# A two-layer hybrid decoder trunk on one core: banks for the latent values, side work in six pieces, and half of layer 2's value weights prepared at the end of layer 1

## The chip, the core and the metric

The kernel runs on one core of a Trainium2 chip. A core has a matrix engine (TensorE, PE), a vector engine (VectorE, DVE), a scalar engine (ScalarE, ACT) and a general engine (GpSimd, POOL); SyncE (SP) issues the DMA transfers here. TensorE writes its results to eight accumulation banks (PSUM), and a bank can take the next result only when the engines that read the last one are done. Each engine works through its own instructions in a fixed order. The metric is the time of one execution on the device, in microseconds (us); less is better.

## What is computed

A sequence of 1024 tokens with 16 learned meta tokens ahead of it (1040 columns in the kernel) goes through two layers. Each layer normalises its input, projects it, runs three kinds of attention beside each other, gates and merges them, and adds an output projection:

```python
def hybrid_layer(x, pos, norm_g, w_in, b_f, g_cq, g_ckv, w_uq, w_ukv, sinks, w_branch, w_out):
    h = rmsnorm(x, norm_g)
    proj = h @ w_in
    (a_q, a_k, a_v, a_f, a_z, b_cq, b_ckv, b_kr, b_z,
     c_q, c_k, c_v, c_z, gates) = jnp.split(proj, np.cumsum(SPLIT_SIZES)[:-1], axis=-1)
    log_f = jax.nn.log_sigmoid((a_f + b_f).astype(jnp.float32))
    log_cum = jnp.cumsum(log_f, axis=1)                    # the forget gate
    y_a = causal_block_attention(a_q, a_k, a_v, FOX_DH ** -0.5, log_cum)
    cq = rmsnorm(b_cq, g_cq)                               # the latent norms
    ckv = rmsnorm(b_ckv, g_ckv)
    qB = (cq @ w_uq)
    kvB = (ckv @ w_ukv)                                    # latent keys and values
    k_rope = rope(b_kr, pos)                               # the shared rotary key
    y_b = causal_block_attention(q_b, k_b, v_b, (MLA_NOPE + MLA_ROPE) ** -0.5)
    y_c = sliding_window_sink_attention(rope(c_q), rope(c_k), c_v, sinks)
    ...
    return x + merged @ w_out
```

The model is 1024 wide; the latent key and value part has 256 channels, the latent query part 384.

## The kernel before

All matrices are 32-bit floats. For TensorE each is split into a rounded high part and the remainder, and each product is three matmuls: high by high, high by low, low by high (`mm3`, L175 to L177; for values L453 to L455). A split of a weight is `split` (L157 and L158): a cast on ScalarE (`wh`, `wvh`) and a subtraction (`wl`, `wvl`) on GpSimd; for activations the subtraction is VectorE's. `weights` loads 1024 columns into a buffer `wr` and splits them; there are two buffers `wr` for all weights, `value_weights` (the weights of the value projections, of 320, 360 and 256 columns for each of the input's 128-row parts, in pieces of up to 1024 columns) uses the same two.

The eight banks are four tags of two: ps_s, ps_pj, ps_t and ps_o. `dense()` gives the next bank out of a rotation, `banks[0]`, which is MOST (ps_s and ps_pj) or ALL (all four). A norm takes its sum of squares and its reciprocal root on ps_t (`rstd`, L189 to L204) and its products on ps_o (`normed`, L212), whatever the rotation is.

A layer goes through these stages:

- **Values.** `values` runs over the eight token blocks of 128 (t) and, for each, over two halves (`wv0`, 320 columns, then `wv1`, 360 columns, which also hold the shared rotary key and the forget gate); at the end over the meta tokens. ScalarE copies the first half to `vst` (L460), VectorE the second (L458), and SyncE stores them.
- **Sliding-window keys and queries, and side work.** The key projection T_CK, then four query columns in two passes (kv). Ahead of pass 0 stand `forget_gates`, ahead of pass 1 `rotary_key` (L550 to L588): small operations of VectorE, ScalarE and SyncE on 8 and 32 rows, for the forget gate's running sum (scans L582, offsets L585, additions L587) and the shared key's rotation.
- **The latent stage.** Projections to the latent channels, their two norms, then `values(vb, 1, ...)` on the normed channels, sixteen blocks of six matmuls of 256 columns, with gate projections (`some`) between; then the latent keys (`wkn`), four pairs in three chunks of 264, 264 and 512 columns. From the end of the norms on the rotation is ALL (`banks[0] = ALL`, ahead of L674).
- Attention, gates, merge. Then the **output projection**: eight columns (d) of three chunks, each followed by the addition of the residual (L1023), its squares and a store to `x_d`. The last two columns are run chunk by chunk, and after each chunk comes the norm of layer 2. Layer 2 then begins with `value_weights` of both halves and `values`.

The order in which an engine gets its instructions is not the program's. A scheduler runs through the program with its own timing and gives each engine the ready instruction that is first in the program; the result is fixed, and on the chip each engine takes it in that order.

Of the kernel before, what the change touches and what calls it, by code (L numbers as in the profile page):

```python
# [11 lines left out]
F32 = mybir.dt.float32  # L12
F32R = mybir.dt.float32r
# [5 lines left out]
P = 128  # L19
# [66 lines left out]
def tile_kernel(ctx: ExitStack, tc, a, out):  # L86
# [320 lines left out]
    def value_weights(pool, srcs, nk, raws=None):  # L407

        ws = []
        for i, src in enumerate(srcs):  # L410
            n = src.shape[1]
            ncol = n // nk
            wh = pool.tile([P, n], F32R, tag=f"wvh{i}", name="wvh")
            wl = pool.tile([P, n], F32R, tag=f"wvl{i}", name="wvl")
# [12 lines left out]
    def values(pool, which, ws, nk, rh, rl, rest=None, between=None):  # L427
# [7 lines left out]
        for t in list(range(NB)) + [-1]:  # L435
            rows = NM if t < 0 else P
            s0 = 0 if t < 0 else NM + t * P
            for half, (wh, wl, ncol) in enumerate(ws):
                o = dense()[:, :ncol]
                st = pool.tile([P, 360], F32, tag="vst", name="vst", bufs=4)  # L440
                if t < 0:
                    for k in range(nk):
                        for i, w in enumerate((wh, wl)):
                            nc.tensor.matmul(o[:48], xm[:, k], w[:, k * ncol:(k + 1) * ncol],
                                             start=(k + i == 0), stop=(k == nk - 1 and i == 1))
                    nc.scalar.copy(st[:NM, :ncol], o[32:48])
                    nc.vector.tensor_tensor(st[:NM, :ncol], o[:NM], st[:NM, :ncol], ALU.add)
                    o = st
                else:
                    for k in range(nk):  # L450
                        xh = rh[:, k, s0:s0 + P]
                        w1 = wh[:, k * ncol:(k + 1) * ncol]
                        nc.tensor.matmul(o, xh, w1, start=(k == 0), stop=False)  # L453
                        nc.tensor.matmul(o, xh, wl[:, k * ncol:(k + 1) * ncol], start=False, stop=False)
                        nc.tensor.matmul(o, rl[:, k, s0:s0 + P], w1, start=False, stop=(k == nk - 1))  # L455
                nv = ncol // DH * DH
                if t >= 0 and half:
                    nc.vector.tensor_copy(st[:, :nv], o[:, :nv])  # L458
                elif t >= 0:
                    nc.scalar.copy(st[:, :nv], o[:, :nv])  # L460
                dma(vm_d[which][:, 2 * half:2 * half + 2] if t < 0 else v_d[which][half, :, t],
                    st[:rows, :256])
                if nv > 256:
                    dma(vc_d[:rows, t + 1, half], st[:rows, 256:320])
# [688 lines left out]
```

## Time and profile before

| | |
|---|---|
| median of 3 runs | 2605.56 us (2605.33 to 2613.88) |
| profiled execution, its own time | 2608.11 us |
| its span, first to last instruction | 2606.3 us |
| TensorE busy | 2535.9 us, 97% |
| VectorE, ScalarE, GpSimd busy | 49%, 46%, 38% |
| mean granted TensorE clock | 0.990 |

The span is that of one profiled execution; 1.8 us of its time lie outside the span. A matmul's busy time is modelled, so two matmuls that follow each other closely overlap in the timeline; their distance is told by their starts. In a timeline the bracket at the end of a row says how long the engine was idle ahead of it, and what ended that.

### The profile page before, as it was taken

The numbers are of one execution on the slowest core, as the hardware profiler recorded it, in microseconds if no ns is written. First come the engines' busy times: TensorE is split into PE (matmuls) and PEld (weight loads), VectorE is DVE, ScalarE is ACT, GpSimd is POOL, SyncE is SP. The second block draws the span as 40 slices with busy tenths as digits, with TensorE's granted clock in tenths as the row PEclk, the third lists the DMA queues.
The fourth block names the chain that finished last, engine by engine and source line by source line (L and its number), as shares of the span: only waits on it lengthen the run. The fifth ranks groups of instructions, "written<-read, shape, count | busy, mean of one in ns | idle before, by whom it ended". The sixth has DMA issues, their size and how long they took to land.

```text
span 2606.3 us, 42099 instructions
## 1 busy us (share of the span) xinstructions
PE 2535.9 (97%) x15446; PEld 2263.1 (87%) x15446; DVE 1283.8 (49%) x3339; ACT 1199.7 (46%) x2684; POOL 993.8 (38%) x966
## 2 busy tenths in 40 slices
PE   8999999999999999999999989999999999999998
PEld 7888899999888999899988878888887888888797
DVE  6464355544263445657156453455334623565643
ACT  5233355545374456644232333455445633566433
POOL 2141545354332424462333325445324341352534
PEclk9999999999999999999999989999999999999999
DMA  5143512222634434364232344222216353453532
GB/s 168 54 136 137 202 46 81 76 74 80 172 103 112 128 102 126 105 223 167 87 101 79 116 156 159 70 82 70 86 69 172 106 158 86 117 148 122 178 130 73
DMA packets 137631, 303.40 MB, mean 116 GB/s; under 512 B 22560, under 2 KB 63296, under 8 KB 137424
## 3 DMA queue, kind: packets, MB, share of 16 engines
q1 hardware_dynamic: 137424, 300.71, 37.5%
q8 instruction: 122, 2.00, 0.3%
q14 instruction: 85, 0.70, 0.1%
HBM read 211.98 MB, written 88.66 MB: 115 GB/s over the span
## 4 chain that ended last, share of the span: by engine, by line
PE 85%; DMA 5%; DVE 5%; ACT 2%; issue 1%; SPq 1%; POOL 1%; POOLq 0%; ACTq 0%; DVEq 0%
PE ps_pj L175 15%; PE ps_pj L176 15%; PE ps_pj L177 15%; PE ps_t L268 5%; PE ps_s L982 3%; PE ps_o L312 3%; PE ps_s L176 3%; PE ps_s L177 3%; PE ps_s L175 2%; PE ps_o L310 2%; PE ps_o L175 2%; PE ps_t L177 2%; PE ps_t L175 2%; PE ps_t L176 2%; PE ps_o L176 2%; PE ps_o L177 2%
## 5 line engine op out<-in xcount | busy, mean ns | idle before, releaser
L158 POOL TENSOR_TENSOR wl<-wr,wh 128x1024 fp32r<-128x1024 f32 (+1 forms) x156 | 373.8, 2397 | 798.1 <-ACT wh L157 667.5
L175 PE MATMUL ps_pj<-hh,wh 128*128 128x512 f32 (+1 forms) x1912 | 672.5, 352 | 5.0 <-DVE zs L718 2.2
L176 PE MATMUL ps_pj<-hl,wh 128*128 128x512 f32 (+1 forms) x1912 | 671.1, 351 | 0.0
L177 PE MATMUL ps_pj<-hh,wl 128*128 128x512 f32 (+1 forms) x1912 | 669.6, 350 | 0.0
L175 PEld LDWEIGHTS ps_pj<-hh,wh 128*128 128x128 f32 x1912 | 362.3, 189 | 47.7 <-DVE zs L718 3.0
L177 PEld LDWEIGHTS ps_pj<-hh,wl 128*128 128x128 f32 x1912 | 362.6, 190 | 41.1 <-issue 0.2
L176 PEld LDWEIGHTS ps_pj<-hl,wh 128*128 128x128 f32 x1912 | 362.4, 190 | 39.9 <-issue 0.5
L158 DVE TENSOR_TENSOR ptl<-ps_t,pth 128x512 fp32r<-128x512 f32 (+1 forms) x386 | 244.7, 641 | 139.3 <-ACT pth L157 132.9
L157 ACT CAST pth<-ps_t 128x512 fp32r<-128x512 f32 (+1 forms) x386 | 205.9, 547 | 170.1 <-PE ps_t L268 140.9
L260 ACT ACTIVATE P<-P,mn 128x656 f32<-128x656 f32 (+8 forms) x272 | 206.9, 761 | 163.9 <-DVE mn L255 159.2
L157 ACT CAST wh<-wr 128x1024 fp32r<-128x1024 f32 (+1 forms) x156 | 162.1, 1039 | 250.4 <-PE ps_pj L176 146.2
L268 PE MATMUL ps_t<-ident,P 128*128 128x128 f32 x1152 | 188.0, 276 | 0.8 <-DVE ptl L158 0.7
L310 PE MATMUL ps_o<-pth,vp 128*128 128x256 f32 (+1 forms) x640 | 167.6, 277 | 2.6 <-DVE u L281 1.4
L312 PE MATMUL ps_o<-ptl,vp 128*128 128x256 f32 (+1 forms) x640 | 159.7, 287 | 2.1 <-DVE ptl L158 1.9
L298 POOL COPY pmeta<-P 128x16 f32<-128x16 f32 x256 | 49.7, 198 | 273.7 <-ACT P L260 270.1
L982 PE MATMUL ps_s<-kt,qt 96*128 96x328 f32 (+9 forms) x696 | 147.8, 330 | 2.9 <-DVE mn L255 2.7
L268 PEld LDWEIGHTS ps_t<-ident,P 128*128 128x128 f32 x1152 | 135.3, 141 | 9.2 <-DVE ptl L158 1.5
L792 POOL TENSOR_TENSOR cm<-ckb,tri 128x128 f32<-128x128 f32 (+1 forms) x136 | 60.5, 447 | 184.9 <-DVE mn L255 181.2
L310 PEld LDWEIGHTS ps_o<-pth,vp 128*128 128x128 f32 x640 | 120.8, 189 | 11.3 <-ACT pth L157 1.9
L312 PEld LDWEIGHTS ps_o<-ptl,vp 128*128 128x128 f32 x640 | 120.5, 188 | 8.8 <-DVE ptl L158 4.7
L281 DVE TENSOR_TENSOR u<-ps_o,hv 64x256 f32<-64x256 f32 x128 | 53.9, 421 | 136.6 <-ACT hv L280 121.5
L982 PEld LDWEIGHTS ps_s<-kt,qt 96*128 96x128 f32 (+1 forms) x696 | 109.2, 188 | 10.1 <-DVE mn L255 5.3
(391 smaller groups left out, 5667.2 us busy)
## 6 DMA issues: line engine op xcount, KB each, us to landing
wr<-in_w_dram SPq DMA_DIRECT2D x108, 512.0 KB
gate_d<-gt SPq DMA_DIRECT2D x72, 256.0 KB
gt<-gate_d SPq DMA_DIRECT2D x24, 520.0 KB
wr<-in_wbr_dram SPq DMA_DIRECT2D x24, 512.0 KB
gt<-gate_d SPq DMA_DIRECT2D x24, 512.0 KB
kn_d<-sg SPq DMA_DIRECT2D x16, 520.0 KB
ckb<-ck_d SPq DMA_DIRECT2D x16, 520.0 KB
kt<-kn_d SPq DMA_DIRECT2D x16, 520.0 KB
```

The costliest lines, as they stand in the source:

```text
L157: nc.scalar.copy(hi, src)
L158: (eng or nc.vector).tensor_tensor(lo, src, _f(hi), ALU.subtract)
L175: nc.tensor.matmul(dst, w1, rh[:, k, c0:c1], start=(k == 0), stop=False)
L176: nc.tensor.matmul(dst, w1, rl[:, k, c0:c1], start=False, stop=False)
L177: nc.tensor.matmul(dst, wl[:, k * P:k * P + m], rh[:, k, c0:c1], start=False, stop=(k == nk - 1))
L260: nc.scalar.activation(s[:rows, :n], s[:rows, :n], AF.Exp, bias=prev, scale=-1.0, accum_out=total)
L268: nc.tensor.transpose(t[:kk, c:c + rows], src, ident[:rows, :rows])
L281: nc.vector.tensor_tensor(u[mine, :n], o[mine, :n], t[mine, :n], ALU.add)
L310: nc.tensor.matmul(dst, vp[:, j + x, vs], ph[:, cols], start=(j + x == 0), stop=False)
L312: nc.tensor.matmul(dst, vp[:, j + x, vs], pl[:, cols], start=False, stop=(diag and x == 1))
L792: nc.gpsimd.tensor_tensor(cm[:rows, :rows], ckb[:rows, d:n], tri[:rows, :rows], ALU.add)
L982: nc.tensor.matmul(dst, q[:, qi, q0:q0 + rows], kt[:, ki, c0:c1], start=(x == 0), stop=(x == 2))
```

## The change

Four things are changed:

- The rotation stays at MOST while the latent values and the latent keys are computed; it becomes ALL after them.
- `forget_gates` and `rotary_key` are one generator, `side_work`, with five stops. One piece is written into the program after each query chunk, the rest after the loop.
- The weights wv0 of layer 2 are loaded and split in the program after column d = 2 of layer 1's output projection, into a pool `vw` of their own that is allocated behind hh and hl and released with layer 2's query stage. Layer 2's start then prepares wv1 alone.
- `values` has its inner part in `block(t, half)`, and with span 2 (layer 2's first values) its order is t0 first half, t1 first half, t0 second half, t1 second half, and so on. The turn of the small columns that each block leaves is taken first in, first out.

```diff
-        for t in list(range(NB)) + [-1]:
+        def block(t, half):
...
-                if half == 0 and due:
-                    due.pop()()
+            if half == 0 and due:
+                due.pop(0)()
...
+        for ts in [range(t, t + span) for t in range(0, NB, span)] + [[-1]]:
+            for half in range(len(ws)):
+                for t in ts:
+                    block(t, half)
+                    if between and half and t % 3 == 1:
+                        between()
...
-            ws = value_weights(va, [a["wv0"][l], a["wv1"][l]], KD)
+            ws = early_ws + value_weights(va, [a["wv1"][l]], KD, at=1)
...
-        values(va, 0, ws, KD, hh, hl, rest)
+        values(va, 0, ws, KD, hh, hl, rest, span=1 if first else 2)
...
-        def rotary_key():
+        def side_work():
...
             nc.scalar.activation(e, e, AF.Ln, bias=ones[:H, 0:1])
+            yield
...
+                if n_ == 4:
+                    yield
+            yield
...
             dma(ck_d, e)
+            yield
...
+            nc.vector.tensor_tensor(r2, krt[32:64], s16[32:64], ALU.mult)
+            yield
...
             for kv in range(2):
-                (rotary_key if kv else forget_gates)()
...
                         split(rows[x][0][:, c0:c1], rows[x][1][:, c0:c1], oo[x], SWA_SCALE)
+                    next(aside, None)
...
+            for _ in aside:
+                pass
         pa.release()
+        if not first:
+            vw.release()
...
-        banks[0] = ALL
 
         with tc.tile_pool(name=f"mq{l}", bufs=2, side=A, reuse_waits="tile") as pm:
             values(vb, 1, ws, 2, cvh, cvl, between=some)
...
                 some()
+            banks[0] = ALL
...
             hl = hpool.tile([P, KD, L], F32R, tag="hl", name="hl")
+            vw = tc.alloc_tile_pool(name=f"vw{l}", bufs=1, side=A, reuse_waits="tile")
...
                     column(d, w, c0, c1)
+                if first and d == 2:
+                    early_ws = value_weights(vw, [a["wv0"][l + 1]], KD)
```

Lines below the values are up to twenty further down in the changed kernel; L453 to L455 become L454 to L456, L458 becomes L459.

The first place is SyncE's queue at the end of layer 1, from the first store of the output projection on. `in_wo_dram` are output weights, `in_wv_dram` layer 2's value weights, `x_d` the stores. Before:

```order
L101 DMA x_d<-xn 128x264
L101 DMA wr<-in_wo_dram 128x1024
L101 DMA x_d<-xn 128x264
L101 DMA x_d<-xn 128x512
L101 DMA x_d<-xn 128x264
L101 DMA wr<-in_wo_dram 128x1024
L101 DMA x_d<-xn 128x264
L101 DMA x_d<-xn 128x512
L101 DMA x_d<-xn 128x264
L101 DMA wr<-in_wo_dram 128x1024
```

and now:

```order
L101 DMA x_d<-xn 128x264
L101 DMA wr<-in_wv_dram 128x960
L101 DMA x_d<-xn 128x264
L101 DMA x_d<-xn 128x512
L101 DMA x_d<-xn 128x264
L101 DMA wr<-in_wv_dram 128x960
L101 DMA x_d<-xn 128x264
L101 DMA wr<-in_wv_dram 128x640
L101 DMA x_d<-xn 128x512
L101 DMA wr<-in_wo_dram 128x1024 x2
```

The three loads of wv0 take the places of the next two wo loads and one more, and two wo loads follow right behind the third; one store of 512 columns stands between.

The second place is the start of layer 2 on TensorE; 320 columns are a first half, 360 a second. Before, the rows around the first matmul of a second half:

```order
L454 MATMUL ps_s<-wvl,hh 128x320
L455 MATMUL ps_s<-wvh,hl 128x320
L453 MATMUL ps_s<-wvh,hh 128x320
L454 MATMUL ps_s<-wvl,hh 128x320
L453 MATMUL ps_pj<-wvh,hh 128x360
L455 MATMUL ps_s<-wvh,hl 128x320
L453 MATMUL ps_s<-wvh,hh 128x320
L454 MATMUL ps_s<-wvl,hh 128x320
```

and now:

```order
L454 MATMUL ps_s<-wvh,hh 128x320
L455 MATMUL ps_s<-wvl,hh 128x320
L456 MATMUL ps_s<-wvh,hl 128x320
L454 MATMUL ps_s<-wvh,hh 128x360
L454 MATMUL ps_s<-wvh,hh 128x320
L455 MATMUL ps_s<-wvl,hh 128x320
L456 MATMUL ps_s<-wvh,hl 128x320
```

The first matmul of a second half is now the 19th row of the stage, where it was the 36th.

The third place is the latent stage of layer 2. On TensorE, from the sixth value block on, before (cvh and cvl are the normed latent channels):

```order
L453 MATMUL ps_pj<-wvh,cvh 128x256
L454 MATMUL ps_pj<-wvl,cvh 128x256
L455 MATMUL ps_pj<-wvh,cvl 128x256
L453 MATMUL ps_pj<-wvh,cvh 128x256
L454 MATMUL ps_pj<-wvl,cvh 128x256
L455 MATMUL ps_pj<-wvh,cvl 128x256
L453 MATMUL ps_t<-wvh,cvh 128x256
L454 MATMUL ps_t<-wvl,cvh 128x256
L455 MATMUL ps_t<-wvh,cvl 128x256
L453 MATMUL ps_t<-wvh,cvh 128x256
```

and now:

```order
L454 MATMUL ps_pj<-wvh,cvh 128x256
L455 MATMUL ps_pj<-wvl,cvh 128x256
L456 MATMUL ps_pj<-wvh,cvl 128x256
L454 MATMUL ps_pj<-wvh,cvh 128x256
L455 MATMUL ps_pj<-wvl,cvh 128x256
L456 MATMUL ps_pj<-wvh,cvl 128x256
L454 MATMUL ps_s<-wvh,cvh 128x256
L455 MATMUL ps_s<-wvl,cvh 128x256
L456 MATMUL ps_s<-wvh,cvl 128x256
L454 MATMUL ps_s<-wvh,cvh 128x256
```

The block after that on ps_pj is on ps_s now instead of the norm's ps_t; from there on ps_s and ps_pj take turns through values and keys. On VectorE the end of the latent query norm (ps_t and ps_o by L201 to L212 and L158) and the copies of the second halves (L458, now L459), before:

```order
L158 TENSOR_TENSOR cql<-ps_o,cqh 128x512
L212 SCALAR_TENSOR_TENSOR ps_o<-raw_16425,gcol,ps_t 128x512 x2
L158 TENSOR_TENSOR cql<-ps_o,cqh 128x512 x2
L212 SCALAR_TENSOR_TENSOR ps_o<-raw_16425,gcol,ps_t 128x512
L158 TENSOR_TENSOR cql<-ps_o,cqh 128x512
L458 COPY vst<-ps_o 128x256
L458 COPY vst<-ps_pj 128x256
L458 COPY vst<-ps_o 128x256
L458 COPY vst<-ps_pj 128x256
L458 COPY vst<-ps_o 128x256
L458 COPY vst<-ps_pj 128x256
L458 COPY vst<-ps_o 128x256
L158 TENSOR_TENSOR sg_16850<-ps_t,sg_16849 128x264
```

and now:

```order
L459 COPY vst<-ps_pj 128x256
L203 TENSOR_TENSOR ps_t<-ps_t,rs_r 128x512
L459 COPY vst<-ps_pj 128x256
L158 TENSOR_TENSOR cql<-ps_o,cqh 128x512
L204 SCALAR_TENSOR_TENSOR ps_t<-ps_t,rs_r 128x512
L459 COPY vst<-ps_pj 128x256
L448 TENSOR_TENSOR vst<-ps_s,vst 16x256
L212 SCALAR_TENSOR_TENSOR ps_o<-raw_16429,gcol,ps_t 128x512 x2
L448 TENSOR_TENSOR vst<-ps_pj,vst 16x256
L158 TENSOR_TENSOR cql<-ps_o,cqh 128x512 x2
L212 SCALAR_TENSOR_TENSOR ps_o<-raw_16429,gcol,ps_t 128x512
L158 TENSOR_TENSOR cql<-ps_o,cqh 128x512
L158 TENSOR_TENSOR sg_16854<-ps_s,sg_16853 128x264
```

Copies that stood in a row behind the norm now stand between its steps; the first split of the latent keys (sg from ps_s) follows the norm's last.

In layer 1 the rows of every engine are the same in both kernels, but for buffer numbers, from the start to the latent stage.

## Rows read from the trace of the kernel before

**Rows 1.** The core's span and mean granted TensorE clock

```profile
core 0: 2606.3 us, clock 0.990
```

**Rows 2.** Busy time by stretch (columns: stretch, PE, PEld, DVE, ACT, POOL, PEclk, DMA, GB/s)

```profile
120.00:140.00 20.00, 15.48 (x80) 13.88 (x79) 19.44 (x43) 6.41 (x11) 11.99 (x10) 0.83 0.34 82
220.00:240.00 20.00, 16.31 (x103) 14.48 (x102) 15.00 (x32) 8.26 (x20) 0.30 (x1) 0.91 0.38 126
1240.00:1300.00 60.00, 60.00 (x400) 55.66 (x399) 9.30 (x19) 14.57 (x23) 25.59 (x20) 1.00 0.28 91
1300.00:1320.00 20.00, 17.63 (x78) 14.18 (x77) 16.95 (x41) 10.38 (x23) 8.72 (x6) 0.91 0.24 70
1320.00:1340.00 20.00, 16.54 (x101) 14.94 (x100) 15.55 (x30) 11.92 (x26) 11.70 (x6) 1.00 0.60 177
1400.00:1420.00 20.00, 20.00 (x88) 16.18 (x87) 20.00 (x46) 6.03 (x11) 11.36 (x7) 1.00 0.31 75
1500.00:1520.00 20.00, 13.22 (x69) 11.16 (x68) 15.94 (x24) 9.08 (x17) 2.40 (x1) 0.73 0.31 100
```

**Rows 3.** What TensorE waited for (us in total, times, longest)

```profile
PE ps_t L453 <- DVE ps_o L212: 8.4, 2, 5.2
...
PE ps_o L175 <- DVE ro L230: 4.5, 1, 4.5
```

**Rows 4.** ScalarE's timeline, layer 1's end (start, us, engine, line, [idle before <-releaser])

```profile
1241.83 1.05 ACT L157 CAST wh<-wr 128x1024 fp32r<-128x1024 f32 x1 [4.38 <-PE ps_o L176]
...
1253.04 1.05 ACT L157 CAST wh<-wr 128x1024 fp32r<-128x1024 f32 x1 [4.27 <-PE ps_t L176]
```

**Rows 5.** SyncE's queue at the end of layer 1

```profile
1226.28 0.38 SPq L101 DMA_DIRECT2D wr<-in_wo_dram  x1
...
1234.54 0.38 SPq L101 DMA_DIRECT2D wr<-in_wo_dram  x1
```

**Rows 6.** GpSimd's timeline at the start of layer 2

```profile
1310.97 4.87 POOL L158 TENSOR_TENSOR wvl<-wr,wvh 128x960 fp32r<-128x960 f32 x2 [3.52 <-ACT wvh L157]
...
1317.03 1.56 POOL L158 TENSOR_TENSOR wvl<-wr,wvh 128x640 fp32r<-128x640 f32 x1 [0.20 <-ACT wvh L157]
```

**Rows 7.** ScalarE's timeline at the start of layer 2, a cast that waited for a load

```profile
1316.23 0.72 ACT L157 CAST wvh<-wr 128x640 fp32r<-128x640 f32 x1 [0.99 <-DMA wr<-in_wv_dram]
```

**Rows 8.** SyncE's queue at the start of layer 2

```profile
1313.22 9.98 SPq L101 DMA_DIRECT2D wr<-in_wv_dram  x4
```

**Rows 9.** TensorE's timeline at the start of layer 2

```profile
1313.25 0.42 PE L454 MATMUL ps_s<-wvl,hh 128*128 128x320 f32 x1 [1.89 <-POOL wvl L158]
...
1328.96 0.43 PE L454 MATMUL ps_pj<-wvl,hh 128*128 128x360 f32 x1 [0.87 <-POOL wvl L158]
...
1335.74 0.39 PE L177 MATMUL ps_t<-hh,wl 128*128 128x264 f32 x1 [1.94 <-POOL wl L158]
...
1337.09 0.39 PE L453 MATMUL ps_pj<-wvh,hh 128*128 128x320 f32 x1
```

**Rows 10.** TensorE's timeline in layer 2's latent stage

```profile
1506.74 0.28 PE L454 MATMUL ps_pj<-wvl,cvh 128*128 128x256 f32 x1
1506.86 0.28 PE L455 MATMUL ps_pj<-wvh,cvl 128*128 128x256 f32 x1
1512.36 0.58 PE L453 MATMUL ps_t<-wvh,cvh 128*128 128x256 f32 x1 [5.22 <-DVE ps_o L212]
...
1512.95 0.41 PE L455 MATMUL ps_t<-wvh,cvl 128*128 128x256 f32 x1
...
1526.29 0.28 PE L175 MATMUL ps_t<-cvh,wh 128*128 128x264 f32 x1
...
1531.96 0.39 PE L175 MATMUL ps_s<-hh,wh 128*128 128x512 f32 x1
```

**Rows 11.** VectorE's timeline in layer 2's latent stage

```profile
1518.21 0.69 DVE L158 TENSOR_TENSOR cql<-ps_o,cqh 128x512 fp32r<-128x512 f32 x1 [0.65 <-ACT cqh L157]
...
1521.45 0.42 DVE L458 COPY vst<-ps_o 128x256 f32<-128x256 f32 x1 [1.89 <-DMA v_d<-vst]
```

More of the change, by code (lines that the diff above doesn't have):

```diff
@@ L412, in value_weights @@
             ncol = n // nk
-            wh = pool.tile([P, n], F32R, tag=f"wvh{i}", name="wvh")
-            wl = pool.tile([P, n], F32R, tag=f"wvl{i}", name="wvl")
+            wh = pool.tile([P, n], F32R, tag=f"wvh{at + i}", name="wvh")
+            wl = pool.tile([P, n], F32R, tag=f"wvl{at + i}", name="wvl")
             step = 1024 // ncol * ncol
@@ L425, in value_weights, with values @@
         return ws
-    def values(pool, which, ws, nk, rh, rl, rest=None, between=None):
+    def values(pool, which, ws, nk, rh, rl, rest=None, between=None, span=1):
         due = []
@@ L434, in values @@
         rounded(xm[:, :, 32:48], _f(rl[:, :, 0:NM]))
-        for t in list(range(NB)) + [-1]:
+        def block(t, half):
+            wh, wl, ncol = ws[half]
             rows = NM if t < 0 else P
             s0 = 0 if t < 0 else NM + t * P
[L438 to L464, printed above, removed]
-                if half == 0 and due:
-                    due.pop()()
-                if ncol > nv:
-                    due.append(rest(t, o[:rows, nv:ncol]))
-            if between and t % 3 == 1:
-                between()
@@ new lines, in block @@
+            o = dense()[:, :ncol]
+            st = pool.tile([P, 360], F32, tag="vst", name="vst", bufs=4)
+            if t < 0:
+                for k in range(nk):
+                    for i, w in enumerate((wh, wl)):
+                        nc.tensor.matmul(o[:48], xm[:, k], w[:, k * ncol:(k + 1) * ncol],
+                                         start=(k + i == 0), stop=(k == nk - 1 and i == 1))
+                nc.scalar.copy(st[:NM, :ncol], o[32:48])
+                nc.vector.tensor_tensor(st[:NM, :ncol], o[:NM], st[:NM, :ncol], ALU.add)
+                o = st
+            else:
+                for k in range(nk):
+                    xh = rh[:, k, s0:s0 + P]
+                    w1 = wh[:, k * ncol:(k + 1) * ncol]
+                    nc.tensor.matmul(o, xh, w1, start=(k == 0), stop=False)
+                    nc.tensor.matmul(o, xh, wl[:, k * ncol:(k + 1) * ncol], start=False, stop=False)
+                    nc.tensor.matmul(o, rl[:, k, s0:s0 + P], w1, start=False, stop=(k == nk - 1))
@@ new lines, in block @@
+            nv = ncol // DH * DH
+            if t >= 0 and half:
+                nc.vector.tensor_copy(st[:, :nv], o[:, :nv])
+            elif t >= 0:
+                nc.scalar.copy(st[:, :nv], o[:, :nv])
+            dma(vm_d[which][:, 2 * half:2 * half + 2] if t < 0 else v_d[which][half, :, t],
+                st[:rows, :256])
+            if nv > 256:
+                dma(vc_d[:rows, t + 1, half], st[:rows, 256:320])
+            if half == 0 and due:
+                due.pop(0)()
+            if ncol > nv:
+                due.append(rest(t, o[:rows, nv:ncol]))
```

29 lines of the change are left out of this document (14 added, 15 removed).

## The prediction

> **What bounds the kernel now.** TensorE does: it is busy in nearly the whole span and its mean granted clock is 0.990 [rows 1], so time can come only from stretches where it waits, or works at 1.2 GHz of its two levels, 1.2 and 2.4 GHz. I read the busy time by stretch first [rows 2]; the reader is to see four places that fall short of 20 us. In 120 to 140 TensorE is busy 15.48 at a clock of 0.83; in 220 to 240, 16.31 at 0.91; in 1300 to 1340, 17.63 and 16.54; in 1500 to 1520, 13.22 at 0.73. Then I asked what ended the waits [rows 3]: 8.4 us in two waits of the latent values for the norm's last step on ps_o, and 4.5 us in layer 1 where TensorE waits for a bank that the rotation holds. The third view is the timeline at each place [rows 4 to 11].
>
> **Side work in six pieces: nothing.** It aims at 120 to 140, where idle time (20 - 15.48 = 4.5) and clock (0.17 x 20 = 3.4) lose 7.9 us. But in layer 1 the order of every engine reads the same up to the latent stage, so VectorE meets the same queue and the stall stays. In layer 2 VectorE's order there does change. TensorE is busy 20.00 in 1400 to 1420 although VectorE is busy 20.00 too [rows 2]: there is nothing to win. The nearest row for a loss is layer 1's stall, 7.9. I take 0, since layer 2 now hides the same operations in any order that VectorE's queue can hold, and the pieces make its bursts shorter.
>
> **Layer 1's end: nothing, if the cover holds.** Three loads, three casts and three splits of wv0 move up beside the output projection. TensorE is busy 60.00 of 60 there, GpSimd 25.59 and ScalarE 14.57 [rows 2]. Per column group there are 11.21 us (1241.83 to 1253.04) [rows 4], and the splits that move are 4.87 + 1.56 = 6.43 us of GpSimd [rows 6]. What counts is the pair of buffers wr, which all loads share, and SyncE's queue, since x_d's stores and the next wo loads stand behind a load that waits for a buffer. The first wv load takes the slot at 1226.28, the second that at 1234.54 [rows 5]. A load lands 3.0 us after its issue (1313.22 to 1316.23) [rows 7, 8]. ScalarE's order has the first cast at about 1234.5, so GpSimd ends the first split at about 1238, and the third load goes out; the second split ends near 1242, and wo of d = 3 is issued. It lands near 1246, and with a cast of 1.05 [rows 4] and a split of 2.4 (half of 4.87) [rows 6] it is ready near 1250. TensorE wants it when it is done with d = 2, which is what the cast at 1253.04 waited for [rows 4]. Slack: 3 us. So 0, by a margin that is a third of a group.
>
> **Layer 2's start: 7.6 gained.** In 1300 to 1340 TensorE loses 20 - 17.63 = 2.4 and 20 - 16.54 = 3.5 of idle time, and 0.09 x 20 = 1.8 of clock [rows 2]: 7.6 us (of unrounded terms). The waits that end last there are all for weights: wvl 1.89 and 0.87, wl 1.94 [rows 9], behind GpSimd's 4.87 us split that begins only at 1310.97 [rows 6] and loads that SyncE issues from 1313.22 on [rows 8]. Afterwards wv0 lies ready, wv1's first two loads stand where wv0's stood, and the key weights follow two places earlier in SyncE's queue. While the t0 and t1 blocks of wv0 run, GpSimd has time for wv1. What is late next is the norm: VectorE is busy 16.95 and 15.55 of 20 there [rows 2], and t2 began at 1337.09 before [rows 9], so it had the normed columns of t1 long before; pulled up by 8 us, they get tight. Blocks of t0 and t1 are interleaved now, so that two halves of t0 and the key projection's first chunk can cover it. Ends: 10 (the refill behind each wait goes too; an estimate from the 1.9 us wait before 1335.74 and the half-speed rows around it) and 4 (idle time of the second window stays). I take 7.6.
>
> **Layer 1's latent values: 5.0 gained.** The loss in 220 to 240 is 20 - 16.31 = 3.7 idle and 0.09 x 20 = 1.8 clock, 5.5 us [rows 2]; 8.4 - 5.2 = 3.2 of it is one wait of values on ps_t for the norm's ps_o [rows 3]. On ps_s and ps_pj alone the values no longer stand behind the norm; TensorE takes gate work between, for which the order has 72 matmuls. What comes last then is VectorE, which is busy 15.00 of 20 [rows 2] and copies each second half out. I take 5.0; the ends are 5.5 and 2, if second halves wait for two norm operations of VectorE each time.
>
> **Layer 2's latent values: 5.5 gained.** From the end of the sixth block, 1506.98, to the first gate at 1531.96 [rows 10] go 25.0 us. The work in it: ten blocks and the meta rows, 68 matmuls of 256 columns at 0.12 (1506.74 to 1506.86), 8.2 us; and two key pairs, 1526.29 to 1531.96, 5.7 us [rows 10]. So 13.9 of work and 11.1 lost: 5.22 in the one wait, and much of the rest by matmuls that come 0.21 apart after it (1512.36 to 1512.95 is two and more at that pace), at 1.2 GHz [rows 10]. Without the banks of the norm TensorE would be through at 1520.9, a gain of 11.1. But VectorE has the norm until 1518.21 + 0.69 = 1518.9 [rows 11], and now the copies among it: five of 0.42 [rows 11] and two meta additions, 2.9 us. The key splits stand behind all of it in its order, so they begin at about 1521. Four banks hold four of the six key results; the other two, 5.7 / 3 = 1.9 us, and a cast and a split follow: the gate starts near 1525, 7.0 earlier. A wait of some 3 us ahead of that may bring the clock down as in 220 to 240, 1.8 us [rows 2], of which I take most: 5.5. Ends: 11.1 and 2 (7.0 less 5, if the clock stays as low as before).
>
> **Sum.** 7.6 + 5.0 + 5.5 = 18.1 us. The profiled execution took 2608.11 (span 2606.3 and 1.8 around it) and would take 2590.0; it lies 2.55 above the median of the runs, so the forecast is 2605.56 - 18.1 = 2587.5.
>
> **Rivals.**
> *Layer 2's start is bound by the norm.* VectorE's 16.95 and 15.55 of 20 [rows 2] and its chain with ScalarE speak for it; that all three large waits there name weights [rows 9] speaks against. Then the 7.6 shrinks to about 0, the sum is 10.5, the time 2595.
> *The output projection starves.* If the three wv pieces run one after another (load 3.0, cast 1.0, split 2.4 each, 19.2 in all) from a first cast at 1234.5 less a load, and wo of d = 3 goes behind them with 6.4 more, its weights come at about 1257 to 1260, up to 7 late, and the clock adds 1.8: 2587.5 + 9 = 2596.5. For it: one pair of buffers, a queue in order. Against: the second load is issued at 1234.54, before the first split ends, so they overlap.
> *The slower side: four banks keep the clock down.* The copies on VectorE now free four banks one by one, so that one long wait becomes many short ones, and both latent stages run at 1.2 GHz throughout. In layer 2 the 13.9 us of work would take 27.8 instead of 25.0, +2.8. In layer 1 the 72 gate matmuls (48 of 264 columns at 0.12 and 24 of 512 at twice that, 11.5) and twelve blocks of six at 0.12 (8.6) would lose 20.1 instead of 5.5, +14.6. With 7.6 from layer 2's start: 2605.56 + 17.4 - 7.6 = 2615. It decides against the change from some 24 us of work at the low level on (7.6 + 5.5 + 11.1). Against it: in rows 10 the clock was full through six blocks on these same two banks, and fell after 5.22 us of idle time.
> The Trainium skill (TensorE: Matmul & The Clock Gate, section "A second HAM failure mode: psum-queue depth-cycling") tells of a kernel that cycles through PSUM banks and lets TensorE idle so often between its groups that the clock goes to and fro. By that rule this rival is what the smaller set of banks would bring, 2615; no row of the trace before shows it for blocks on ps_s and ps_pj.
> *It does more than the order shows:* the six pieces remove layer 1's stall as well, 18.1 + 7.9, 2580. Since the order is the same, hardly.
>
> **How the numbers follow.** Forecast 0.68, norm-bound start 0.16, starved projection 0.09, low clock 0.05, the last 0.02. The forecast's own ends are 10 + 5.5 + 9 = 24.5 (2581; 11.1 needs VectorE free) and 4 + 2 + 2 = 8 (2597.5). The range is 2580 to 2600: it holds the first three cases nearly whole and leaves the low clock and the tails out. A measurement of this kernel tells about 0.5%, 13 us, from no change: faster means below 2592.5. Of the forecast's 0.68 I put 0.59 below that; with the last case faster has 0.61. Same: the rest of the forecast and the two rivals at 2595 and 2596.5, with most of the low clock, 0.35. Slower by over 0.5% is 0.04, a low clock with a loss at layer 1's end.
>
> **What would show it.** In the profile after: the wait of L453's successor on ps_o gone from the list of TensorE's waits; the stretches of the two latent stages at a granted clock above 0.95; the waits for wvl and wl at layer 2's start gone, and TensorE busy over 19 of 20 in both windows; 60 of 60 still at layer 1's end; the 4.5 us wait in layer 1 unchanged. I am wrong if TensorE waits for hl or for VectorE's splits of sg for more than 5 us, if a wait for wl shows up near 1250, or if the clock falls in a new place.

## The result

| | before | after |
|---|---|---|
| median of the runs | 2607.64 us (6 runs, 2604.68 to 2613.88) | 2588.45 us (6 runs, 2587.49 to 2592.05) |
| profiled execution, its own time | 2608.11 us | 2592.05 us |
| its span | 2606.3 us | 2590.3 us |
| mean granted clock | 0.990 | 0.993 |

The ratio is 0.9927 (95% interval 0.9913 to 0.9940): the change makes the kernel 0.7% faster, 19.2 us between the medians. The forecast was 2587.5 us. One execution of the kernel before took 12860.57 us where the other eight of its series took 2600 to 2610; it is left out of the ratios that rest on that series.

Both kernels run the same 15,446 matmuls, and TensorE's order differs only in the two latent stages, at layer 1's end and from layer 2's start to its queries. So I matched them by their number and took how much earlier each starts in the profiled execution of after. The lead is 5.0 us behind layer 1's latent stage and 5.0 again at layer 1's end; it grows by 9.4 at layer 2's start, falls by 1.7 where the queries begin, and grows by 4.9 in layer 2's latent stage: 17.6 us. From there it wanders up to 20.1, falls by 4.0 in one place near the end and ends at 16.1.

The profile after, busy time by stretch, the same stretches as in [rows 2] (stretch, PE, PEld, DVE, ACT, POOL, PEclk, DMA, GB/s):

```profile
120.00:140.00 20.00, 15.46 (x82) 13.87 (x81) 19.45 (x42) 6.43 (x11) 11.99 (x10) 0.83 0.35 82
220.00:240.00 20.00, 20.00 (x141) 18.45 (x140) 15.39 (x32) 8.80 (x20) 1.85 (x1) 1.00 0.45 133
1240.00:1300.00 60.00, 60.00 (x388) 55.07 (x387) 11.74 (x25) 15.60 (x26) 24.33 (x19) 1.00 0.31 99
1300.00:1320.00 20.00, 20.00 (x117) 18.57 (x116) 17.72 (x42) 12.01 (x26) 10.91 (x8) 1.00 0.41 125
1320.00:1340.00 20.00, 20.00 (x135) 19.93 (x135) 12.92 (x25) 7.60 (x22) 3.58 (x2) 1.00 0.39 116
1500.00:1520.00 20.00, 16.95 (x89) 14.16 (x88) 11.76 (x23) 6.03 (x14) 0.00 (x0) 0.91 0.57 214
```

The four rows that fell short in [rows 2] are 15.46, 20.00, 20.00 and 20.00, and 16.95 of 20 now. The first is unchanged; in the last some of the loss is left, with a clock of 0.91. In what TensorE waited for (us, times, longest) the 8.4 us of [rows 3] are gone. Four lines are new or larger by over 1.3 us: the second to the fourth here, and a wait for VectorE's u in layer 1's attention (2.8 us, 1.1 before), though the lead is about 5.0 ahead of that attention and behind it:

```profile
PE ps_o L175 <- DVE ro L230: 4.5, 1, 4.5
PE ps_s L175 <- ACT m L157: 3.7, 1, 3.7
...
PE ps_s L175 <- DVE sg L158: 2.4, 1, 2.4
...
PE ps_pj L177 <- POOL wl L158: 1.4, 1, 1.4
```

The 2.4 us are the wait for VectorE's split of the first latent key, and it is where the prediction had it, behind the norm's last split. TensorE and VectorE there:

```profile
1510.54 0.39 PE L175 MATMUL ps_s<-cvh,wh 128*128 128x264 f32 x1 [2.38 <-DVE sg L158]
...
1512.51 0.63 PE L176 MATMUL ps_pj<-cvl,wh 128*128 128x512 f32 x1
...
1513.37 0.63 PE L175 MATMUL ps_s<-hh,wh 128*128 128x512 f32 x1
```

```profile
1509.45 0.69 DVE L158 TENSOR_TENSOR cql<-ps_o,cqh 128x512 fp32r<-128x512 f32 x1 [0.65 <-ACT cqh L157]
1510.06 0.42 DVE L158 TENSOR_TENSOR sg<-ps_s,sg 128x264 fp32r<-128x264 f32 x1
```

TensorE waits 2.38 us from 1508.15 on; some 1.5 us after it has begun again, matmuls of 512 columns come 0.42 apart (1512.09 to 1512.51), the low clock, until 1515.3. The first gate starts at 1513.37, where it was 1531.96 [rows 10]: 18.6 us earlier, of which 12.8 were brought along and 5.8 gained here; the low clock then takes 0.9.

At layer 1's end GpSimd's split of the fourth column's weights, and the cast that waits for TensorE to be done with the third, as in [rows 4]:

```profile
1243.47 2.40 POOL L158 TENSOR_TENSOR wl<-wr,wh 128x1024 fp32r<-128x1024 f32 x1 [1.82 <-ACT wh L157]
```

```profile
1248.00 1.05 ACT L157 CAST wh<-wr 128x1024 fp32r<-128x1024 f32 x1 [4.27 <-PE ps_t L176]
```

The weights are there at 1245.87 and TensorE wants them at 1248.0: 2.1 us to spare, and 60.00 of 60 us busy. The 1.7 us that are given back lie in layer 2's query stage, in a wait that the kernel before did not have, behind a split on GpSimd:

```profile
1415.48 0.50 PE L177 MATMUL ps_pj<-hh,wl 128*128 128x512 f32 x1 [1.39 <-POOL wl L158]
```

The 3.7 us for m (the input of the output projection, 1.1 us in the profiled execution before) are in a part whose order is the same in both kernels, near the end of layer 2. It is there that the lead falls from 20.1 to 16.1: 2.6 us by the wait and 1.5 behind it, at a granted clock of 0.91 in 2480 to 2500. The same wait took 1.1 to 2.0 us in the four kernels here that load wv0 at layer 2's start, and 1.4 to 3.7 in the ten that load it early, 2.9 or more in eight of them; what sets it was not tried.

### The profile page after: what moved, and what is told of

Same layout as the page of the kernel before. It is cut to its first block, busy times and chain, and to the rows that moved or that the text cites. A ratio compares the mean times of both kernels' runs of the same rounds, so it can differ in the third digit from the quotient of the medians.

```text
span 2590.3 us, 42110 instructions
## 1 busy us (share of the span) xinstructions
PE 2527.6 (98%) x15446; PEld 2256.7 (87%) x15446; DVE 1286.9 (50%) x3339; ACT 1199.9 (46%) x2684; POOL 996.0 (38%) x966
## 4 chain that ended last, share of the span: by engine, by line
PE 77%; DMA 5%; DVE 4%; ACT 2%; issue 2%; POOL 1%; SPq 1%; POOLq 0%; ACTq 0%; DVEq 0%
PE ps_pj L175 14%; PE ps_pj L176 14%; PE ps_pj L177 14%; PE ps_t L268 5%; PE ps_s L999 3%; PE ps_o L312 3%; PE ps_o L310 2%; PE ps_s L176 2%; PE ps_s L175 2%; PE ps_s L177 2%; PE ps_s L804 1%; PE ps_s L802 1%; PE ps_o L176 1%; PE ps_o L175 1%; PE ps_o L177 1%
## 5 line engine op out<-in xcount | busy, mean ns | idle before, releaser
L158 POOL TENSOR_TENSOR wl<-wr,wh 128x1024 fp32r<-128x1024 f32 (+1 forms) x156 | 376.6, 2414 | 838.3 <-ACT wh L157 712.2
L158 DVE TENSOR_TENSOR ptl<-ps_t,pth 128x512 fp32r<-128x512 f32 (+1 forms) x386 | 244.7, 641 | 140.6 <-ACT pth L157 134.3
```

Of the source, the lines that this page charges most:

```text
L158: (eng or nc.vector).tensor_tensor(lo, src, _f(hi), ALU.subtract)
```

## The experiments

Times are medians, ratios are to the kernel before on the same chip, with their 95% intervals. How a kernel stands to the changed one (ratio 0.9927) is taken from the two ratios, 0.001 being 2.6 us, since chips differ. "Lead" is the distance of matched matmuls as above.

### Each part alone

**The banks alone**, in the kernel before:

```diff
-        banks[0] = ALL
         with tc.tile_pool(name=f"mq{l}", bufs=2, side=A, reuse_waits="tile") as pm:
             values(vb, 1, ws, 2, cvh, cvl, between=some)
...
+            banks[0] = ALL
             c16 = pm.tile([P, L], F32, tag="c16", name="c16", bufs=1)
```

> The kernel before with only the rotation kept on ps_s and ps_pj for the latent values and keys. Theory (the places add up): TensorE comes 4.9 us earlier out of layer 1's latent stage and 4.9 out of layer 2's, nothing else moves: 9.8 us less than before, ratio 0.996, and the wait for ps_o is gone from TensorE's list. Rival (fewer banks keep the clock low): the granted clock of the two latent stages falls below 0.9 and the gain is under 4 us.

2592.68 us, ratio 0.9953 (0.9939 to 0.9966). The lead grows by 5.0 in layer 1's latent stage and by 6.5 in layer 2's. Layer 2's stretch:

```profile
1500.00:1520.00 20.00, 16.44 (x117) 14.80 (x116) 16.64 (x32) 9.39 (x22) 0.00 (x0) 1.00 0.61 207
```

The wait for the key's split is there, 2.4 us as after, but the clock was 1.00: the 1.6 us between 6.5 and 4.9 are what the low clock took after, where 3.4 us (1511.8 to 1515.3) ran at half speed. So the theory holds, and layer 2's gain is 4.9 or 6.5 as the clock falls behind the 2.4 us wait or does not. Two traces with the same order can differ by that much in one stage.

**The early load and the pairs of blocks alone:**

```diff
-            ws = value_weights(va, [a["wv0"][l], a["wv1"][l]], KD)
+            ws = early_ws + value_weights(va, [a["wv1"][l]], KD, at=1)
...
-        values(va, 0, ws, KD, hh, hl, rest)
+        values(va, 0, ws, KD, hh, hl, rest, span=1 if first else 2)
...
+                if first and d == 2:
+                    early_ws = value_weights(vw, [a["wv0"][l + 1]], KD)
```

> The kernel before with only the early load and split of wv0 and the blocks taken two by two. Theory: 9.4 us gained at layer 2's start, 1.7 given back where the queries begin, 7.7 us less than before, ratio 0.997; TensorE busy 60.00 of 60 us at layer 1's end. Rival (the gain at the start hangs on the rest of the change): under 4 us. Rival (the output projection starves): a wait for wl of the fourth column of several us.

2597.42 us, ratio 0.9967 (0.9954 to 0.9979), 8.6 us. By lead 9.4 at layer 2's start less 1.7 in the query stage. The two parts' ratios together make 0.9920, the change 0.9927: the parts add up.

**The six pieces alone:**

```diff
-                (rotary_key if kv else forget_gates)()
...
+                    next(aside, None)
...
+            for _ in aside:
+                pass
```

> The kernel before with only the side work written in six pieces. The order of every engine's instructions is the same as before, so the theory says 0 us, ratio 1.000 within its interval, and the wait of 4.5 us in layer 1 stays. Rival (something that the order does not show, such as where tiles lie, moves it): a difference of over 3 us.

2608.37 us, ratio 1.0008 (0.9999 to 1.0018). No difference, and TensorE's waits are those of [rows 3]:

```profile
PE ps_t L453 <- DVE ps_o L212: 8.4, 2, 5.2
...
PE ps_o L175 <- DVE ro L230: 4.5, 1, 4.5
```

The scheduler gives each engine the same rows whether the side work stands in two calls or in six pieces, in layer 2 as well. Where the side work stands in the program did not matter to it here.

### Layer 2's start: the load or the pairs?

**The changed kernel with wv0 loaded late again**, the pairs kept:

```diff
-            ws = early_ws + value_weights(va, [a["wv1"][l]], KD, at=1)
+            ws = value_weights(va, [a["wv0"][l], a["wv1"][l]], KD)
...
-                if first and d == 2:
-                    early_ws = value_weights(vw, [a["wv0"][l + 1]], KD)
```

> The changed kernel with wv0 of layer 2 loaded and split at layer 2's start again, the blocks still two by two. Theory (the weights are what TensorE waits for at layer 2's start): the 9.4 us there are gone, or go below zero since second halves are asked for earlier; 8 to 12 us more than the changed kernel, ratio to before 0.996. Rival (the new order of the blocks brings the gain): at most 4 us more than the changed kernel.

2594.12 us, ratio 0.9961 (0.9948 to 0.9974): 8.9 us more than the changed kernel. The waits for weights of [rows 9] are back, the first of them whole, the later ones shorter:

```profile
1303.19 0.41 PE L455 MATMUL ps_s<-wvl,hh 128*128 128x320 f32 x1 [1.89 <-POOL wvl L158]
...
1310.44 0.43 PE L454 MATMUL ps_s<-wvh,hh 128*128 128x360 f32 x1 [0.58 <-ACT wvh L157]
...
1325.34 0.39 PE L177 MATMUL ps_t<-hh,wl 128*128 128x264 f32 x1 [0.63 <-POOL wl L158]
```

By lead the start gains 3.6 instead of 9.4, so 5.8 of the 8.9 us are shown there. The theory holds in the main; what it left out is that the pairs alone give over a third, and not a loss.

**The changed kernel without the pairs**, wv0 early:

```diff
-        values(va, 0, ws, KD, hh, hl, rest, span=1 if first else 2)
+        values(va, 0, ws, KD, hh, hl, rest, span=1)
```

> The changed kernel with the early load of wv0 but each block's two halves one behind the other. Theory (both are needed): TensorE is through the first half of t0 in 3.5 us, and wv1's last piece is split some 8 us after layer 2's start, so 3 to 5 of the 9.4 us are lost again, in waits for wvl. Rival (the early load alone brings the gain, and the scheduler fills with other blocks): within 1.5 us of the changed kernel.

2586.41 us, ratio 0.9933 (0.9914 to 0.9952): 1.6 us more than the changed kernel, which their intervals don't tell from none. The lead at the start grows by 9.2, nearly the same, with no wait for wvl, so the theory fell there. But the query stage gives back 4.8 instead of 1.7, most of it in one wait:

```profile
1407.15 0.80 PE L177 MATMUL ps_s<-hh,wl 128*128 128x512 f32 x1 [3.13 <-POOL wl L158]
```

Without the pairs the queries come up on a weight split sooner; the pairs are worth some 3 us there by this one trace. The time leaves open which expectation is nearer.

### How much cover layer 1's end has

**The early load done twice:**

```diff
-                    early_ws = value_weights(vw, [a["wv0"][l + 1]], KD)
+                    for _ in range(2):
+                        early_ws = value_weights(vw, [a["wv0"][l + 1]], KD)
```

> The changed kernel with the early load and split of wv0 done twice, one behind the other (the second result is the one used). In the changed kernel the weights of the fourth output column are ready 2.1 us before TensorE needs them. Theory (the cover at layer 1's end is two shared buffers and SyncE's queue, and it is nearly used up): three more pieces of about 3 to 4 us each exceed it, TensorE waits 4 to 10 us for wl at the fourth column, and the time is 4 to 12 us above the changed kernel's. Rival (the engines there are idle enough to take it): no wait, within 2 us of the changed kernel.

2594.58 us, ratio 0.9956 (0.9939 to 0.9974), 7.6 us above the changed kernel. TensorE waits for the fourth column, for the cast and then for the split, and the clock falls:

```profile
1248.66 0.59 PE L175 MATMUL ps_o<-m,wh 128*128 128x264 f32 x1 [4.29 <-ACT wh L157]
...
1251.10 0.59 PE L177 MATMUL ps_o<-m,wl 128*128 128x264 f32 x1 [0.34 <-POOL wl L158]
```

```profile
1240.00:1260.00 20.00, 15.37 (x78) 13.25 (x77) 1.56 (x3) 5.07 (x8) 13.48 (x9) 0.83 0.46 155
```

7.8 us of lead are lost there. GpSimd is busy only 13.48 of 20 us and ScalarE 5.07, and ScalarE's casts wait for loads:

```profile
1244.73 0.72 ACT L157 CAST wvh<-wr 128x640 fp32r<-128x640 f32 x1 [3.85 <-DMA wr<-in_wv_dram]
...
1247.56 1.04 ACT L157 CAST wh<-wr 128x1024 fp32r<-128x1024 f32 x1 [1.57 <-DMA wr<-in_wo_dram]
```

So the queue of loads behind two buffers is what ran out, not an engine. Three more pieces used up the 2.1 us to spare and cost 4.6 us of waits on top.

### Banks and the clock

**Latent values on two banks:**

```diff
+            banks[0] = ("s",)
             values(vb, 1, ws, 2, cvh, cvl, between=some)
+            banks[0] = MOST
```

> The changed kernel with the latent values on ps_s alone, two banks instead of four; the latent keys as in the changed kernel. Theory (the change pays because values no longer stand behind the norm's banks): with two banks a block waits for the copy of the one before the last, 0.7 us of work against copies of 0.4 behind norm operations of up to 1.4, so short waits of 3 to 8 us in the two stages together, and the granted clock stays above 0.9 outside of waits of over 2 us. Rival (fewer banks make many short waits that keep the clock at its low level): the clock of both stages falls to 0.8 or below, 10 us or more than the changed kernel.

2585.62 us, ratio 0.9929 (0.9913 to 0.9944): no slower than the changed kernel. The two stretches, and TensorE's waits in layer 2's:

```profile
220.00:240.00 20.00, 19.98 (x130) 17.86 (x129) 15.86 (x34) 9.48 (x22) 1.84 (x1) 1.00 0.38 108
1500.00:1520.00 20.00, 19.24 (x106) 16.20 (x106) 9.55 (x20) 6.00 (x14) 0.00 (x0) 1.00 0.61 214
```

```profile
1494.12 0.38 PE L454 MATMUL ps_s<-wvh,cvh 128*128 128x256 f32 x1 [0.27 <-DVE vst L459]
...
1496.37 0.39 PE L454 MATMUL ps_s<-wvh,cvh 128*128 128x256 f32 x1 [0.56 <-DVE vst L459]
...
1498.57 0.39 PE L454 MATMUL ps_s<-wvh,cvh 128*128 128x256 f32 x1 [0.50 <-ACT vst L461]
...
1505.44 0.32 PE L445 MATMUL ps_s<-wvh,xm 128*48 128x256 f32 x1 [0.72 <-DVE vst L459]
```

TensorE waits 0.3 to 0.7 us at a time for the copies, 2.0 us in these four, and the granted clock is 1.00 in both stretches. That is less than the 3 to 8 us that the theory put on such waits. Layer 1's stage loses 1.3 us of lead against the changed kernel, layer 2's wins 2.6, since the values come later and the keys then find VectorE free. Fewer banks made short waits, and these short waits did not bring the clock down.

**The latent keys on all eight banks**, the values on four:

```diff
+            banks[0] = ALL
             wh, wl = weights(a["wkn"][l], 1024)
...
-            banks[0] = ALL
             c16 = pm.tile([P, L], F32, tag="c16", name="c16", bufs=1)
```

> The changed kernel with the rotation back on all eight banks for the latent keys alone, the values still on ps_s and ps_pj. In the changed kernel the keys wait 2.4 us in layer 2 for VectorE's split of the first key, behind the norm. Theory (VectorE's queue is what ends last there, not the banks): the wait stays between 1 and 3.5 us, now partly as a wait for ps_o, and the time is within 2 us of the changed kernel. Rival (more banks for the keys bridge the wait): 2.4 us and the clock's fall behind it vanish, 3 to 4 us less.

2582.68 us, ratio 0.9918 (0.9901 to 0.9936), 2.3 us less than the changed kernel, with intervals that overlap. The trace shows where:

```profile
1500.00:1520.00 20.00, 20.00 (x109) 17.25 (x108) 9.50 (x19) 8.30 (x18) 1.86 (x1) 1.00 0.56 205
```

```profile
1497.23 0.29 PE L175 MATMUL ps_t<-cvh,wh 128*128 128x264 f32 x1
...
1501.28 0.39 PE L175 MATMUL ps_s<-hh,wh 128*128 128x512 f32 x1
...
1507.77 0.29 PE L175 MATMUL ps_o<-cvh,wh 128*128 128x264 f32 x1
```

```profile
1504.76 0.69 DVE L158 TENSOR_TENSOR cql<-ps_o,cqh 128x512 fp32r<-128x512 f32 x1 [0.65 <-ACT cqh L157]
1505.37 0.42 DVE L158 TENSOR_TENSOR sg<-ps_t,sg 128x264 fp32r<-128x264 f32 x1
```

TensorE is busy 20.00 of 20 at full clock and the wait of 2.4 us is gone, as the rival had it; the stage gains 10.6 us of lead, 5.7 more than in the changed kernel, of which some 1.6 is the low clock that the changed kernel's trace has there and this one has not. By the times the edit is not told from none. VectorE comes to the first key no sooner with regard to its norm. But the first key can go to ps_t, which the norm is done with, and the scheduler now puts the next gate (hh, wh at 1501.28, 24 matmuls) behind the first pair of keys; the second pair begins at 1507.77, when VectorE is through. The wait is filled with other work.

### Layer 1's stall: the additions, or where they stand?

The stall of 4.5 us in layer 1 is there in both kernels. VectorE in the kernel before, where TensorE waits for its ro behind these rows:

```profile
126.07 4.08 DVE L587 TENSOR_SCALAR fe<-fe,off 8x128 f32<-8x128 f32 x3
```

and of these three the middle one by itself:

```profile
126.26 3.68 DVE L587 TENSOR_SCALAR fe<-fe,off 8x128 f32<-8x128 f32 x1
```

and GpSimd there:

```profile
126.28 1.28 POOL L232 TENSOR_TENSOR ro<-ro,ro 64x512 f32<-64x512 f32 x1 [2.09 <-DVE ro L229]
127.53 2.34 POOL L158 TENSOR_TENSOR wl<-wr,wh 128x1024 fp32r<-128x1024 f32 x1
```

Three additions of the forget gate, 8 rows each, took 4.08 us, while five others took 1.06. The first and the third took 0.27 us as the five did; the second alone took 3.68. It ends when GpSimd's two operations end, at 129.9.

**The additions on ScalarE**, in the changed kernel:

```diff
-                nc.vector.tensor_scalar(e[:, c0:c1], e[:, c0:c1], off[:, n_:n_ + 1], None, ALU.add)
+                nc.scalar.activation(e[:, c0:c1], e[:, c0:c1], AF.Identity, bias=off[:, n_:n_ + 1])
```

> The changed kernel with the forget gate's nine additions of offsets done by ScalarE instead of VectorE, in both layers. In the changed kernel three of them take 4.08 us where GpSimd splits a weight, and TensorE waits 4.5 us for VectorE behind them. Theory (these three stand behind GpSimd's split): the 4.5 us wait in layer 1 and the clock's fall behind it go, as does layer 2's 1.4 us wait for wl: 6 to 9 us less than the changed kernel, ratio to before 0.990. Rival (VectorE is full there whatever it holds; the additions themselves are nine of 0.21 us): at most 2 us less than the changed kernel, the wait stays at 2.5 us or more.

2583.71 us, ratio 0.9913 (0.9898 to 0.9929): 3.7 us less than the changed kernel, between the two expectations. By lead 3.7 in layer 1 and 0.8 in layer 2. The wait for ro is gone, and two shorter ones have taken its place:

```profile
127.37 0.39 PE L175 MATMUL ps_pj<-hh,wh 128*128 128x264 f32 x1 [0.90 <-ACT wh L157]
...
129.81 0.39 PE L177 MATMUL ps_pj<-hh,wl 128*128 128x264 f32 x1 [1.34 <-POOL wl L158]
```

```profile
123.41 2.46 ACT L587 ACTIVATE fe<-fe,off 8x128 f32<-8x128 f32 x8 [2.60 <-DVE off L585]
...
126.28 1.04 ACT L157 CAST wh<-wr 128x1024 fp32r<-128x1024 f32 x1
```

```profile
127.87 2.43 DVE L158 TENSOR_TENSOR sg<-ro,sg 64x512 fp32r<-64x512 f32 x1
```

Eight additions of 2.46 us on ScalarE now stand ahead of the weights' cast, and GpSimd's split follows late; and on VectorE another operation, the key's low part (0.67 us beside nothing), took 2.43 beside that split.

**One addition in place of nine**, on VectorE, with the keys on eight banks:

```diff
-            for n_, (c0, c1) in enumerate(cuts):
-                nc.vector.tensor_scalar(e[:, c0:c1], e[:, c0:c1], off[:, n_:n_ + 1], None, ALU.add)
+            body = e[:, NM:].rearrange("p (t c) -> p t c", c=P)
+            nc.vector.tensor_tensor(body, body, off[:, 1:NB + 1].unsqueeze(2).to_broadcast([H, NB, P]), ALU.add)
```

> The changed kernel with the latent keys on all eight banks, and the forget gate's offsets added by VectorE in one addition over 8 x 1024 in place of nine (the first, of zero, is left out). Theory (VectorE's small additions are held while GpSimd splits a weight, which is why three of 0.21 took 4.08 us): one addition is held at most once, so TensorE's 4.5 us wait shrinks to 2 us or less, or goes where the addition comes ahead of GpSimd's split; 8 to 12 us less than the changed kernel, ratio 0.988. Rival (VectorE's number of operations does not matter, it is full): the wait stays above 3.5 us and the time is that of the keys' edit alone, 0.9918.

2584.00 us, ratio 0.9914 (0.9901 to 0.9927): no gain over the keys' edit alone, and TensorE waits 3.87 us.

```profile
131.27 0.59 PE L175 MATMUL ps_o<-hh,wh 128*128 128x264 f32 x1 [3.87 <-DVE ro L230]
```

```profile
124.33 1.21 DVE L587 TENSOR_TENSOR fe<-fe,off 8x1024 f32<-8x1024 f32 x1
...
126.41 4.00 DVE L158 TENSOR_TENSOR sg<-ro,sg 64x512 fp32r<-64x512 f32 x1
```

```profile
126.28 1.28 POOL L232 TENSOR_TENSOR ro<-ro,ro 64x512 f32<-64x512 f32 x1 [2.24 <-DVE ro L229]
127.52 2.34 POOL L158 TENSOR_TENSOR wl<-wr,wh 128x1024 fp32r<-128x1024 f32 x1
```

The addition takes 1.21 us and is out of the way at 125.5. Now sg, 0.67 us elsewhere, takes 4.00: it begins 0.13 us after a GpSimd operation has begun and ends 0.55 us behind the end of the next. So it is neither the number of the additions (only one of them was held in the first place) nor that VectorE is full, as the rival had it, though its number came out. First an addition and then sg stood at that place, and each was held until GpSimd was through.

The Trainium skill (SBUF — State Buffer, section "Who interferes with whom") says that a VectorE instruction with two inputs in SBUF, or in a mode that uses two ports, shares ports with GpSimd, and that the one that issues first has them for its whole instruction. The traces agree for sg, which has two inputs in SBUF (4.00, 2.43). For the addition (3.68) no trace shows the mode it was in, and its start lies 0.02 us ahead of GpSimd's, too close to tell who issued first. The traces add that one instruction can be held over two of GpSimd's that follow each other, 126.28 to 129.86.

**Both edits that helped**, the keys on eight banks and the additions on ScalarE:

> The changed kernel with two more edits together: the latent keys on all eight banks, and the forget gate's additions on ScalarE. Theory (they act at different places, 4.7 us in layer 1's and layer 2's query stages, 6 us in layer 2's latent stage): 9 to 11 us less than the changed kernel, ratio to before 0.988. Rival (what one frees is spent in the other's queue, since ScalarE also casts the keys): no better than the keys' edit alone, 0.9918.

2579.25 us, ratio 0.9896 (0.9880 to 0.9911), 8.1 us less than the changed kernel, and 1.0% faster than the kernel before. It is the fastest of all kernels here, and its interval does not touch that of the change. The edits' ratios alone would make 6.0 us; within their intervals they add up, a little short of the 9 to 11 that was expected. In layer 1 the additions on ScalarE bring 2.2 us of lead here, and 3.7 in the kernel with that edit alone: behind the same two waits, of 0.9 and 1.3 us, the clock fell here (0.91 in 120 to 140) and stayed up there (1.00).

**And the key's low part on GpSimd too:**

```diff
-                    split(rows[x][0][:64, c0:c1], rows[x][1][:64, c0:c1], oo[x])
+                    split(rows[x][0][:64, c0:c1], rows[x][1][:64, c0:c1], oo[x], eng=nc.gpsimd)
```

> The changed kernel with the latent keys on all eight banks, the forget gate's additions on ScalarE, and the low parts of the sliding-window key (sg from ro, 64 rows) subtracted by GpSimd instead of VectorE. Whichever VectorE operation with its data in SBUF came beside GpSimd's weight split was held until that ended: three additions (4.08 us), one merged run's sg (4.00), one sg with the additions on ScalarE (2.43). Theory (the place, not the operation, is what costs): with sg on GpSimd too no VectorE operation there lasts over 1.5 us; TensorE's two waits of 0.9 and 1.3 us in layer 1 shrink to 1.5 in sum, 1 to 3 us less than without this edit, ratio 0.9885. Rival (GpSimd is the next bound): its queue grows by 5 us in 115 to 135, the wait for wl grows beyond 2 us, and the time is 0 to 5 us above that without this edit, ratio 0.990 to 0.992.

2582.22 us, ratio 0.9901 (0.9884 to 0.9917): not to be told from the one without it, and no better. TensorE waits three times instead of twice in layer 1, 2.0 in sum where it was 2.3:

```profile
127.49 0.39 PE L175 MATMUL ps_pj<-hh,wh 128*128 128x264 f32 x1 [0.27 <-ACT wh L157]
...
128.70 0.39 PE L175 MATMUL ps_o<-hh,wh 128*128 128x264 f32 x1 [0.70 <-DVE ro L230]
...
130.21 0.59 PE L177 MATMUL ps_pj<-hh,wl 128*128 128x264 f32 x1 [1.00 <-POOL wl L158]
```

Behind these three the clock fell, though none is longer than 1.0 us:

```profile
130.00:132.00 2.00, 1.79 (x8) 1.79 (x9) 0.43 (x1) 0.00 (x0) 2.00 (x3) 0.50 0.92 203
```

In layer 2 a wait for wl of 2.2 us has come, where it was 0.5. GpSimd has taken VectorE's place, as the rival said.

## Why the prediction was right

- **The six pieces, 0.** Right, and for more reason than was given. The text let them change VectorE's order in layer 2; alone they change no row there either. What changed it were the other parts, by moving the work's time. The stall in layer 1 stayed at 4.5 us.
- **Layer 1's end, 0.** Right. The walk put the fourth column's weights 3 us ahead of need, the trace 2.1. Loading twice cost 4.6 us of waits and 7.6 in all. By estimate that is (4.6 + 2.1) / 3 = 2.2 us a piece, so a single piece more would have used up the cover: the rival of a starved projection was that near.
- **Layer 2's start, 7.6.** It gained 9.4, near the upper end of 10. The step that was short is the reading of idle time from busy time: a matmul of 320 columns counts as busy for 0.31 us while the next begins 0.15 behind it, so that a gap after each goes uncounted. Counted from start to start in the trace before, such gaps come to 1.2 us there, and what is lost between close matmuls, mostly by the low clock, to some 2.3 more than after, where the sum had 1.8. In two other kernels with the same order there (the banks alone, the six pieces alone) the start took 1.4 and 1.6 us longer still, so 9.4 is the low end of what the change is worth there. 1.7 were given back in the query stage, which the text did not foresee, so 7.7 remain: that this is the 7.6 of the sum is luck, one miss against another. That it is the weights and not the norm that bound it was right: with weights early TensorE is busy 20.00 of 20 in both stretches while VectorE is still busy 17.72 and 12.92. That both the load and the pairs were needed was not: the load alone has 9.2.
- **Layer 1's latent values, 5.0.** It gained 5.0. No waiting for VectorE's copies took anything back.
- **Layer 2's latent values, 5.5.** It gained 4.9, by the way that the text gives: TensorE reaches the keys, fills four banks, and waits for VectorE's first key split behind the norm, 2.4 us where 3 was estimated, with a fall of the clock behind it. The gate came 5.8 us earlier, not 7.0, since VectorE reached the first key some 1.8 us later than estimated; the low clock then took 0.9, not 1.5. With the banks alone, in the same order there, the clock stayed up and the gain was 6.5. One sign that the text gave did not come: it wanted both latent stages above a clock of 0.95, and layer 2's shows 0.91. That did not fit its own sum, which had taken off 1.5 us for the clock.
- **What was missed there:** the text took the wait behind VectorE as given. With the keys on eight banks the same queue of VectorE cost nothing, since the scheduler then had a place for the first key and put a gate behind the first pair. The change keeps the keys off the norm's banks longer than it pays: 5.7 us of lead by one trace, 2.3 us by the times, where the intervals overlap.
- **The rivals.** A norm-bound start and a starved projection did not come about. In the latent stages the low clock came only behind the one wait of 2.4 us. The Trainium skill's case of a kernel that cycles through banks (TensorE: Matmul & The Clock Gate, "A second HAM failure mode: psum-queue depth-cycling") was not met there: with two banks and waits of 0.3 to 0.7 us the clock was 1.00. Waits of up to 1.0 us in layer 1, of another cause and closer together, did bring it down in the last experiment (0.50 in 130 to 132).
- **The median.** The forecast was made from 2605.56; six runs of before have a median of 2607.64. The profiled executions differ by 16.1 us and the medians by 19.2, so 18.1 lies between them. The parts, less what the query stage gave back, add up to 17.6 us of lead; what comes behind them, up 2.5 and down 4.0, the text did not look at.

## What to carry to other kernels

Where a stage's results wait for banks that a slower stage holds, give the two stages banks of their own, but give them back as soon as the slower stage nears its end: the values were well kept off the norm's banks, the keys, by the trace, were not. Weights for the next stage can be prepared under a stage in which TensorE is fully busy; here the queue of loads and the two shared buffers told how much fits, not how busy the engines were. Under a scheduler that orders by readiness, cutting work into pieces in the program may move nothing, as here: compare the order before believing in such a change.

## What the hardware showed that was not expected

A VectorE operation of 0.67 us lasted 4.00, and one addition of 0.27 us lasted 3.68, next to GpSimd, over two GpSimd operations and not only one; taking the additions away moved the hold to another VectorE operation with its data in SBUF (4.00, 2.43). And waits of 0.3 to 0.7 us every 2.2 us or so left the granted clock at 1.00, while after one wait of 2.4 us it fell in some executions (0.91 over 20 us) and not in others (1.00) of the same order of work. And behind three waits of 0.27, 0.70 and 1.00 us in layer 1 it fell as well (0.50 over 2 us).
